# Mixture-of-experts stage of a two-layer model: two weight units split ahead of each border between experts, token products before the lists, one branch fewer

## The chip, the cores and the metric

The kernel runs on one core of one Trainium2 chip. The metric is the device time of one execution in microseconds (us). Five engines work side by side, each through its own list of instructions in order: PE multiplies matrices, DVE and ACT work on vectors and on activations, POOL does the slower elementwise work and issues gathers and scatters, SP issues loads. They wait for one another through semaphores.

## The reference, cut to what matters

Two layers on 512 tokens of width 1024. The stage that is changed is the expert layer of the first layer's second half: every token goes to the two best of eight experts, and an expert is a gated product of inner width 1408.

```python
D_MODEL = 1024
SEQ = 512
D_FF = 11 * D_MODEL // 4
N_EXPERTS = 8
TOP_K = 2
D_FF_EXPERT = D_FF // 2

def swiglu(x, w1, w3, w2):
    return (jax.nn.silu(x @ w1) * (x @ w3)) @ w2
```

The result of a token is the sum over its two experts of gate times `swiglu` with that expert's weights. All of it is float32.

## The kernel before, in words

**Products.** A float32 operand is split into a high part (`hi`, L76, on ACT) and a low part (`lo`, L79, on DVE, which subtracts the high part from the value); a product is three matmuls, low by high, high by low and high by high (L121 to L123). So every weight passes ACT and then DVE before PE can use it.

**Order and queues.** The code is written in one order; a scheduler then sets each engine's list, and `pin` keeps an instruction at its place. At run time each engine goes through its list in order.

**Weights.** An expert has 18 units of weights, 12 of them for the first two products (`w13`) and 6 for the last (`w2`); a unit is 1 MB at most. SP loads them through a ring of six places (`Stream.load`, L1216). `Stream.take` splits the next unit into tiles `wh` and `wl`, each half a unit, out of a pool of four pairs, and then lets SP load the unit six further on. One unit is outside this: the first unit of the next expert is split ahead into the tile `pre`, by `then()`, near the end of the expert before. With one block of tokens, a 1 MB unit is 12 matmuls of 512 columns on PE, two instructions on ACT and two on DVE.

**Experts and arms.** The experts are taken in order of their token counts. Each has three arms: one block of up to 128 tokens, a block and a half (the half block's products are folded, L1522, L1523), or two blocks. Two branches (L1698, L1701) choose the arm from a number, `codei`, that DVE works out and every engine loads (`values_load`). A `hint` ahead of each branch tells the sequencer which arm will come. In the profiled execution the experts 0, 2, 3, 5 and 6 have one block, and 1, 4 and 7 a block and a half. I call the change from expert e-1 to expert e border e. At a border ACT and DVE each copy half of the expert's output `y` out of PE's accumulators (L1625, L1626), go through the jump at the end of the arm (L1701), and then split the second unit of the next expert, in pieces of 512 columns (`fine`).

**Ahead of expert 0.** The normalised tokens come from PE as `pxn`; ACT and DVE split them into `nh` and `nl` (L1407, L1408), in two halves of the width (`hf`). `lists()` sorts the experts by size on DVE, ends with `codei`, and scatters the token lists with eight DMAs from POOL (L1352). `sums` are POOL's eight additions `nh+nl` (L1409), whose results ACT writes to `xn_d` with four DMAs (L1429); the gathers for the later experts read them. Expert 0's own tokens are picked by matmuls with one-hot matrices: 64 products `pO` (L1414, L1415), split into `xg` by ACT and DVE. Before, `lists()`, the split of `pre` and POOL's first four sums stand between the two halves.

**Behind expert 7.** A last branch (label `spill`, L1708) leads to code for more tokens than two blocks hold; all engines pass it before PE's `pyo` (L1733), which puts expert 7's rows back in place, and DVE's `y2` stage (L1735).

Of the kernel before, what the change touches and what calls it, by code (L numbers as in the profile page):

```python
# [48 lines left out]
class Core:  # L49
# [34 lines left out]
        self.nc.sync.dma_start(r, src)  # L84
        return self.split(r, k, n, dst, pin, eng, alone)

    def split(self, r, k, n, dst=None, pin=False, eng=None, alone=False, fine=False):

        kp = -(-k // 2)
        hs, ls = [], []  # L90
        for k0 in range(0, k, kp):
            s, m = k0 * n, (min(k0 + kp, k) - k0) * n
            if dst:
                h, l = (d[:, s:s + m] for d in dst)
            else:
                h = self.wpool.tile([128, 1024], FR, tag="wh", name="wh")[:, :m]
                l = self.wpool.tile([128, 1024], FR, tag="wl", name="wl")[:, :m]
            step = n if fine else m
            for c in (slice(o, o + step) for o in range(0, m, step)):
                q = r[:, s + c.start:s + c.stop]  # L100
                a = eng.tensor_copy(h[:, c], q) if alone else self.hi(h[:, c], q)
                b = self.lo(l[:, c], q, h[:, c], eng)
                self.last_split = a, b
                if pin:
                    self.tc.keep_in_program_order(a)
                    self.tc.keep_in_program_order(b)
            hs.append(h.rearrange("p (k n) -> p k n", n=n))
            ls.append(l.rearrange("p (k n) -> p k n", n=n))
        return Parts(hs, kp), Parts(ls, kp)
# [1066 lines left out]
    def _moe(self, m1, m2):  # L1176
# [33 lines left out]
        class Stream:  # L1210
# [7 lines left out]
            def take(st, late=False, **kw):  # L1218
                i = st.taken
                st.taken += 1  # L1220
                _, k, w = unit(*st.units[i])
                got = self.split(ring[(st.place + i) % 6][:, :k * w], k, w, **kw)
                if i + 6 < len(st.units) and not late:
                    st.load(i + 6)
                return got

        main = Stream([(e, n) for e in range(NE) for n in range(18)], 0)
        for i in range(3):
# [99 lines left out]
                pin(v.tensor_scalar(key[:, 1:], rank[:, 1:], float(r), -7 * 256.0, op0=OP.is_ge, op1=OP.mult))  # L1328
                pin(v.tensor_tensor(lam[:, 1:], lam[:, 1:], key[:, 1:], op=OP.add))

        def lists():
            sort()
            pin(v.tensor_scalar(t1, pos, 256.0, 2048.0 - 256.0, op0=OP.is_ge, op1=OP.mult))
            pin(v.tensor_tensor(t1, t1, lam[:, None, :].to_broadcast([128, 4, 8]), op=OP.add))
# [15 lines left out]
            for j in range(2):  # L1350
                for i in range(4):
                    st = g.indirect_dma_start(out=self.list_d[:, :],  # L1352
                                              out_offset=bass.IndirectOffsetOnAxis(ap=lii[:, j, i:i + 1], axis=0),
                                              in_=self.tid[:, i:i + 1], in_offset=None)
                    for o in scat:
                        tc.declare_no_dep(st.ins, o.ins, reason="every slot is written once")
                    scat.append(st)
            g.dma_start(lst, self.list_d.rearrange("(p c) o -> p (c o)", p=128))
            by = lambda t: t[:, None, :].to_broadcast([128, 8, 8])
            for src, dst in ((rc[:, 1], order), (cnt, None)):  # L1360
# [26 lines left out]
        def hint(e, after={}):  # L1387

            for t in mybir.ALL_ENGINES:
                with tc.issue_after(after[t].ins) if t in after else nullcontext():  # L1390
                    tc.mark_branch_hint_location(f"expert{e}" if e < NE else "spill", (code >> 3 * e + 2) & 1 if e < NE else 0,
                                                 engines=(t,))

        O = [self.bank("pp", "pO") for _ in range(3)] + [self.bank("pt", "pO")]
        for o in O:
            mm(o, self.z1[0:1].to_broadcast([1, 128]), self.z1[0:1].to_broadcast([1, 512]), start=True, stop=False)
        for hf in range(2):
            c = slice(512 * hf, 512 * hf + 512)
            ps, sums = [], []
            for i in range(4):  # L1400
                p = self.bank("pc", "pxn")
                mm(p, ident, rn[:, i, 4 * hf:4 * hf + 4, 0:128], start=True, stop=False)
                mm(p, rows[:, i * 128:(i + 1) * 128], self.gb[:, c], start=False, stop=True)
                ps.append(p)
            for i in range(4):
                col = rs[:, i:i + 1]
                nc.scalar.activation(nh[i][:, c], ps[i], AF.Copy, scale=col)  # L1407
                pin(v.scalar_tensor_tensor(nl[i][:, c], ps[i], col, nh[i][:, c].bitcast(FT), op0=OP.mult, op1=OP.subtract))  # L1408
                sums.append(lambda i=i, c=c: g.tensor_tensor(xn[:, i, c], nh[i][:, c].bitcast(FT), nl[i][:, c].bitcast(FT), op=OP.add))  # L1409
                for k in range(4):  # L1410
                    kk = 4 * hf + k
                    o = O[kk // 2][:, kk % 2 * 256:kk % 2 * 256 + 256]
                    ks = slice(kk * 128, kk * 128 + 128)
                    mm(o, nh[i][:, ks], hot[:, i], start=False, stop=False)  # L1414
                    mm(o, nl[i][:, ks], hot[:, i], start=False, stop=(i == 3 and k % 2 == 1))  # L1415
                if hf and i == 1:
                    code = nc.values_load(codei[0:1, 0:1], min_val=0, max_val=8 ** NE - 1)
                    hint(0)
            if not hf:
                lists()  # L1420
                main.take(dst=pre, pin=True, late=True)
            for add in sums:
                add()
            for j in range(2 * hf, 2 * hf + 2):
                th, tl = (XG[0][:, a, 2 * j:2 * j + 2].rearrange("p k b n -> p (k b n)") for a in range(2))
                self.hi(th, O[j])
                pin(self.lo(tl, O[j], th))
# [70 lines left out]
        def expert(e, blocks, xt, weights, start=None, nxt=None, first=(), then=None, extra=None, half=None):  # L1498
# [46 lines left out]
            for cc in range(6):  # L1545
# [16 lines left out]

                for u in range(2):
                    ahead = first and cc == u == 0
                    w = first if ahead else weights.take(pin=bool(mine) and cc == 1, fine=bool(first) and cc == 0)
                    for b in blocks:
                        if ahead and b and mine:
                            turn(mine, xt, 1, rows[1])
                        product(w, u, b)
# [15 lines left out]
            for u in range(6):  # L1585
# [12 lines left out]
                                      start=(kk == 0), stop=(kk == 10))  # L1598
                if u == 0:
                    flush(5, "pc")  # L1600
                if u == 3 and not over:
                    hint(e + 1, {mybir.EngineType.PE: last, mybir.EngineType.Activation: self.last_split[0],
                                 mybir.EngineType.DVE: self.last_split[1], mybir.EngineType.SP: weights.loaded})
                if nxt and u == (4 if e == 0 else 2):
# [51 lines left out]
                                         in_offset=bass.IndirectOffsetOnAxis(ap=ri[:, j, i:i + 1], axis=0))  # L1656
                    v.scalar_tensor_tensor(xn[:, i], d, wt[:, j, i:i + 1], xn[:, i], op0=OP.mult, op1=OP.add)

        first = [Parts([p.rearrange("p (k n) -> p k n", n=512)], 4) for p in pre]
        for e in range(NE):  # L1660
            if e == NE - 1:

                lo = m1.tile([128, 4, D], FT, tag="xg0", name="ylo")
                hi = [m2.tile([128, D], FT, tag=t, name="yhi") for t in ("y", "y", "xg", "xg")]
                for i in range(4):
                    for j, d in ((1, lo[:, i]), (0, hi[i])):
                        g.indirect_dma_start(out=d, out_offset=None, in_=self.y_d[0:1792, :],
                                             in_offset=bass.IndirectOffsetOnAxis(ap=rwi[:, j, i:i + 1], axis=0))
                start = None

                def nxt(_):
# [3 lines left out]
            else:  # L1675
                start = lambda e=e: fetch((0, 1) if e == NE - 2 else (0,), e + 1)
                nxt = lambda xs, e=e: turn(xs, XG[(e + 1) % 2])

            def then(e=e):
                if e + 1 < NE:  # L1680
                    main.take(dst=pre)
                    main.load(main.taken + 4)

            if e:
                for k in (e, min(e + 1, NE - 1)):
                    which(k)
            at, known = main.taken, dict(regs)
            extra = {1: gates, 3: rows_of_last}.get(e)
            arm_e = (code >> 3 * e) & 3

            def arm(a):
                main.taken = at
                regs.clear()
                regs.update(known)
                expert(e, (0, 1) if a else (0,), XG[e % 2], main, start, nxt, first, then, extra, 1 if a == 1 else None)


            with tc.If(arm_e == 1 - likely[e], preferred_fallthrough_block=False) as other:  # L1698
# [1 line left out]
            with other.Else():  # L1700
                with tc.If(arm_e > 1, label=f"expert{e}", preferred_fallthrough_block=True) as full:  # L1701
                    arm(2)
                with full.Else():
                    arm(likely[e])
            regs.clear()
            regs.update(known)

        with tc.If((code >> 3 * (NE - 1)) & 3 == 3, label="spill"):  # L1708
            others = Stream([(e, n) for e in range(NE) for n in range(18)], main.taken)
            for i in range(6):  # L1710
                others.load(i)
            xt = m1.tile([128, 2, 8, 2, 128], FR, tag="xg0", name="xg")
            for e in range(NE):
                spill(e, others, xt)


        y2 = m1.tile([128, 4, D], FT, tag="xg0", name="y2")
# [662 lines left out]
```

## Time and profile before

| | |
|---|---|
| time, median of 3 executions | 2525.89 us (2522.98 to 2527.27) |
| profiled execution: its own time / its span | 2531.56 us / 2529.7 us |
| mean granted TensorE clock | 0.955 |
| busy share of the span: PE, DVE, ACT, POOL | 93%, 67%, 47%, 19% |
| expert stage in the span | 1107.60 to 1670.00 us |

The span goes from the first to the last instruction of the profiled execution. PE is busy nearly all the time over the whole span; the expert stage takes 562 us of it. The shares are means over stages of different kinds, so the expert stage is read by itself, and there border by border.

### The profile page before, as it was taken

The page shows a single profiled execution, that of the slowest core. Times are in us where ns is not written, and L with a number is a line of the kernel's source. Part 1 is how long each engine was busy: PE and PEld are TensorE (multiplying, and loading weights), DVE is VectorE, ACT ScalarE, POOL GpSimd, SP SyncE. Part 2 cuts the span into 40 slices and gives each one's busy share as a digit, 9 for nine tenths or more (in the row PEclk, how much of TensorE's full clock was granted, in tenths as well). Part 3 has the DMA queues.
Part 4 walks back from the last instruction along what each step waited for, and adds up shares of the span by engine and source line. Part 5 has one row for each costly group of instructions (what it writes and reads, how often), then busy time and mean ns, then how long its engine had stood idle before and what let it go on. Part 6 is the DMA issues. An engine that isn't in the chain of part 4 may idle for free. (4 is left out here: it accounts for less than half of the span.)

```text
span 2529.7 us, 34883 instructions
## 1 busy us (share of the span) xinstructions
PE 2347.8 (93%) x12559; PEld 1901.6 (75%) x12559; DVE 1703.1 (67%) x3585; ACT 1193.1 (47%) x2155; POOL 473.5 (19%) x599
## 2 busy tenths in 40 slices
PE   8999998978999889988989998969999998999997
PEld 7899988866788867756767776758776778787776
DVE  5877668768854774366677677685786557578465
ACT  5544434322333423245565666545555445546453
POOL 1010123665676201030000000110001022001103
PEclk9999999989999899979999999989999998999998
DMA  4323222556645662256678588714131222223111
GB/s 162 112 79 96 62 84 101 202 176 217 236 167 196 183 176 82 102 183 260 230 292 317 175 307 326 280 60 147 55 104 61 95 84 90 79 75 104 59 51 67
DMA packets 107629, 375.34 MB, mean 148 GB/s; under 512 B 23202, under 2 KB 49218, under 8 KB 77448
## 3 DMA queue, kind: packets, MB, share of 16 engines
q1 hardware_dynamic: 73440, 285.86, 32.9%
q0 software_dynamic: 13552, 61.18, 7.0%
q10 hardware_dynamic: 20408, 25.48, 3.0%
q8 instruction: 115, 1.88, 0.3%
q14 instruction: 114, 0.93, 0.1%
HBM read 335.76 MB, written 36.72 MB: 147 GB/s over the span
## 5 line engine op out<-in xcount | busy, mean ns | idle before, releaser
L79 DVE TENSOR_TENSOR wl<-raw,wh 128x1024 fp32r<-128x1024 f32 (+4 forms) x248 | 295.3, 1194 | 202.5 <-ACT wh L76 198.4
L76 ACT ACTIVATE wh<-raw 128x1024 fp32r<-128x1024 f32 (+5 forms) x262 | 245.9, 947 | 285.0 <-PE pp L115 86.4
L79 DVE TENSOR_TENSOR wl<-ring,wh 128x1024 fp32r<-128x1024 f32 (+1 forms) x280 | 297.2, 1099 | 104.9 <-ACT wh L76 102.4
L115 PE MATMUL pp<-xl,wh 128*128 128x512 f32 (+1 forms) x944 | 350.1, 372 | 4.3 <-DVE xl L79 4.3
L114 PE MATMUL pp<-xh,wh 128*128 128x512 f32 (+1 forms) x944 | 349.7, 377 | 4.2 <-ACT wh L76 1.5
L116 PE MATMUL pp<-xh,wl 128*128 128x512 f32 (+1 forms) x944 | 347.8, 370 | 0.0
L76 ACT ACTIVATE wh<-ring 128x1024 fp32r<-128x1024 f32 (+1 forms) x280 | 256.3, 955 | 114.2 <-issue 45.9
L114 PEld LDWEIGHTS pp<-xh,wh 128*128 128x128 f32 x944 | 180.8, 194 | 38.2 <-issue 3.1
L115 PEld LDWEIGHTS pp<-xl,wh 128*128 128x128 f32 x944 | 182.6, 194 | 33.1 <-DVE xl L79 5.1
L116 PEld LDWEIGHTS pp<-xh,wl 128*128 128x128 f32 x944 | 182.4, 193 | 28.4 <-issue 1.8
L121 PE MATMUL ph<-wh,xg 128*128 128x512 f32 (+1 forms) x352 | 139.2, 407 | 30.1 <-ACT wh L76 30.0
L116 PE MATMUL pf<-xh,wl 128*128 128x512 f32 (+1 forms) x384 | 145.6, 380 | 4.4 <-DVE wl L79 4.4
L115 PE MATMUL pf<-xl,wh 128*128 128x512 f32 (+1 forms) x384 | 146.0, 381 | 1.5 <-DVE xl L79 1.5
L114 PE MATMUL pf<-xh,wh 128*128 128x512 f32 (+1 forms) x384 | 145.7, 381 | 1.1 <-ACT wh L76 0.6
L122 PE MATMUL ph<-wl,xg 128*128 128x512 f32 (+1 forms) x352 | 139.2, 395 | 1.8 <-DVE wl L79 1.8
L123 PE MATMUL ph<-wh,xg 128*128 128x512 f32 (+1 forms) x352 | 136.7, 389 | 0.0
L121 PEld LDWEIGHTS ph<-wh,xg 128*128 128x128 f32 x352 | 69.4, 201 | 46.4 <-ACT wh L76 34.1
L1832 DVE SCALAR_TENSOR_TENSOR adaacc<-adaraw,sc,adaacc 128x512 f32<-128x512 f32 x84 | 90.0, 1072 | 18.9 <-DMA adaraw<-w_ada 17.8
L1894 ACT ACTIVATE s<-s,sst 128x128 f32<-128x128 f32 (+3 forms) x128 | 71.0, 557 | 35.8 <-DVE sst L1892 34.0
L116 PEld LDWEIGHTS pf<-xh,wl 128*128 128x128 f32 x384 | 74.3, 194 | 17.7 <-DVE wl L79 4.8
L1479 POOL DMA_INDIRECT xgn<-xn_d,lst x10 | 11.1, 1109 | 402.5 <-PE pxg L1491 392.4
L1902 ACT ACTIVATE PT<-ptp 128x128 f32<-128x128 f32 (+3 forms) x128 | 51.8, 434 | 73.3 <-PE ptp L1899 58.4
(743 smaller groups left out, 5687.4 us busy)
## 6 DMA issues: line engine op xcount, KB each, us to landing
ring<-moe SPq DMA_DIRECT2D x120, 1024.0 KB, 6.1
raw<-w_in SPq DMA_DIRECT2D x30, 1024.0 KB, 4.8
adaraw<-w_ada POOLq DMA_DIRECT2D x24, 1024.0 KB
raw<-w SPq DMA_DIRECT2D x22, 1024.0 KB, 4.8
ring<-moe SPq DMA_DIRECT2D x24, 512.0 KB, 5.4
raw<-w SPq DMA_DIRECT2D x16, 704.0 KB, 3.9
raw<-w_glu SPq DMA_DIRECT2D x8, 1024.0 KB, 4.9
raw<-w_out SPq DMA_DIRECT2D x8, 1024.0 KB, 5.0
```

Source lines behind the costliest of these rows:

```text
L76: return self.nc.scalar.activation(dst, src, AF.Copy, **kw)
L79: return (eng or self.nc.vector).tensor_tensor(dst, src, hi.bitcast(FT), op=OP.subtract)
L114: mm(ps, wh, xh, start=start, stop=False)
L115: mm(ps, wh, xl, start=False, stop=False)
L116: return mm(ps, wl, xh, start=False, stop=stop)
L121: mm(ps, ah, wh, start=start, stop=False)
L122: mm(ps, ah, wl, start=False, stop=False)
L123: return mm(ps, al, wh, start=False, stop=stop)
L1479: g.indirect_dma_start(out=x, out_offset=None, in_=self.xn_d[:, :], in_offset=bass.IndirectOffsetOnAxis(ap=lst[:, q:q + 1], axis=0))
L1832: v.scalar_tensor_tensor(acc, r[:, k], s, acc, op0=OP.mult, op1=OP.add)
L1894: nc.scalar.activation(s, s, AF.Exp, scale=-1.0, bias=st[:, 0:1], accum_out=st[:, 1:2])
L1902: nc.scalar.activation(dst, src, AF.Copy)
```

## The change

1. **Two units ahead.** `then()` also takes the second unit of the next expert. It goes into one of four fixed pairs of tiles (`halves`), used in turn (`turned`) and kept over the arms. For expert 0 the second unit is taken before the token products. The pieces of 512 columns move from the second unit to the third.
2. **Token products whole.** All eight `nh` and `nl` come first, then `lists(sums)` and `pre`, then all 64 products. POOL does the eight scatters before the eight sums.
3. **No last branch.** The spill code moves into the full arm of expert 7, and so do the gathers and additions of the earlier rows into its arms.

```diff
-    def split(self, r, k, n, dst=None, pin=False, eng=None, alone=False, fine=False):
+    def split(self, r, k, n, dst=None, pin=False, eng=None, alone=False, fine=False, into=()):
...
+            elif into:
+                h, l = (d[:, :m] for d in into[len(hs)])
...
+                if "dst" not in kw:
+                    n = min(k, 2)
+                    kw["into"] = [halves[(turned[0] + j) % 4] for j in range(n)]
+                    turned[0] += n
...
+        halves = [[self.wpool.tile([128, 1024], FR, tag=t, name=t) for t in ("wh", "wl")] for _ in range(4)]
+        turned = [0]
...
-        def lists():
+        def lists(sums):
...
+            for dst, a, b in sums:
+                pin(g.tensor_tensor(dst, a, b, op=OP.add))
             g.dma_start(lst, self.list_d.rearrange("(p c) o -> p (c o)", p=128))
...
-                sums.append(lambda i=i, c=c: g.tensor_tensor(xn[:, i, c], nh[i][:, c].bitcast(FT), nl[i][:, c].bitcast(FT), op=OP.add))
+                sums.append((xn[:, i, c], nh[i][:, c].bitcast(FT), nl[i][:, c].bitcast(FT)))
+        lists(sums)
+        main.take(dst=pre, pin=True, late=True)
+        for hf in range(2):
+            for i in range(4):
...
-            if not hf:
-                lists()
-                main.take(dst=pre, pin=True, late=True)
-            for add in sums:
-                add()
...
-                    w = first if ahead else weights.take(pin=bool(mine) and cc == 1, fine=bool(first) and cc == 0)
+                    w = first[u] if first and cc == 0 else weights.take(pin=bool(mine) and cc == 1,
+                                                                        fine=bool(first) and cc == 1 and u == 0)
...
-                if u == 3 and not over:
+                if u == 3 and not over and e + 1 < NE:
...
-        first = [Parts([p.rearrange("p (k n) -> p k n", n=512)], 4) for p in pre]
+        begun = [Parts([p.rearrange("p (k n) -> p k n", n=512)], 4) for p in pre]
+        first = [begun, main.take()]
...
+            def then(e=e):
+                if e + 1 < NE:
+                    main.take(dst=pre)
+                    main.load(main.taken + 4)
+                    later.append(main.take())
...
+                    if e == NE - 1:
+                        with tc.If(arm_e == 3):
+                            others = Stream([(eo, n) for eo in range(NE) for n in range(18)], main.taken)
...
                 with full.Else():
                     arm(likely[e])
+            if later:
+                first = [begun, later[-1]]
...
-        with tc.If((code >> 3 * (NE - 1)) & 3 == 3, label="spill"):
```

The order of the instructions shows what that moves. First DVE, at the end of expert 2 and the start of expert 3's full arm as it stands in the program (border 3; the jump marks the border). The names: `wl` and `pre` are low parts of weights, `xg` of tokens, `hb` the gated products. Before:

```order
L79 TENSOR_TENSOR wl<-ring,wh 128x1024 x4
L1391 REGISTER_ALU x2
L2376 BRANCH_PREFETCH_HINT
L79 TENSOR_TENSOR wl<-ring,wh 128x1024 x2
L79 TENSOR_TENSOR xg<-pxg,xg 128x4x128 x2
L79 TENSOR_TENSOR wl<-ring,wh 128x1024
L1626 COPY y<-py 128x512 x2
L1701 UNCONDITIONAL_BRANCH
L79 TENSOR_TENSOR wl<-ring,wh 128x512 x4
```

Now:

```order
L79 TENSOR_TENSOR wl<-ring,wh 128x1024 x4
L1403 REGISTER_ALU x2
L2397 BRANCH_PREFETCH_HINT
L79 TENSOR_TENSOR wl<-ring,wh 128x1024 x2
L79 TENSOR_TENSOR xg<-pxg,xg 128x4x128 x2
L79 TENSOR_TENSOR wl<-ring,wh 128x1024 x3
L1638 COPY y<-py 128x512 x2
L1720 UNCONDITIONAL_BRANCH
```

Two low parts of 1024 columns, the next expert's second unit, now stand ahead of the copies of `y`; four pieces of 512 columns are gone from behind the jump. (The lists show the arm with two blocks; the copies are one for an engine in the arm that runs.) Next ACT, at a border into an arm with a block and a half (`sl` is the activation, `folds` the folded half block). Before:

```order
L1625 ACTIVATE y<-py 128x512 x2
L1631 DMA y_d<-y 128x1024 x2
L1701 UNCONDITIONAL_BRANCH
L76 ACTIVATE wh<-ring 128x512 x4
L1577 ACTIVATE sl<-ph 128x256
L76 ACTIVATE xg<-pxg 128x4x64 x2
L1522 ACTIVATE folds<-ph 64x512
L1577 ACTIVATE sl<-folds 64x256
L76 ACTIVATE wh<-ring 128x1024 x4
```

Now:

```order
L1637 ACTIVATE y<-py 128x512 x2
L1643 DMA y_d<-y 128x1024 x2
L1720 UNCONDITIONAL_BRANCH
L1589 ACTIVATE sl<-ph 128x256
L76 ACTIVATE xg<-pxg 128x4x64 x2
L1533 ACTIVATE folds<-ph 64x512
L1589 ACTIVATE sl<-folds 64x256
L76 ACTIVATE wh<-ring 128x512 x4
L76 ACTIVATE wh<-ring 128x1024 x2
```

The first weights that ACT splits behind the jump stand behind the fold now, and they are the third unit. Last POOL, between the token products and expert 0's branches. Before:

```order
L1409 TENSOR_TENSOR xn<-nh,nl 128x512 x4
L1352 DMA list_d<-tid,lii 4096x1 x8
L1417 TENSOR_LOAD codei
L1409 TENSOR_TENSOR xn<-nh,nl 128x512 x4
L1358 DMA lst<-list_d 128x32
```

Now:

```order
L1362 DMA list_d<-tid,lii 4096x1 x8
L1369 TENSOR_TENSOR xn<-nh,nl 128x512 x8
L1433 TENSOR_LOAD codei
L1370 DMA lst<-list_d 128x32
```

The first four sums have moved from ahead of the scatters to behind them; ACT's four DMAs to `xn_d` read the sums, and on ACT they now stand behind all four `xg` and ahead of expert 0's branches, as before.

## Rows read from the trace of the kernel before

**Rows 1.** Window of expert 3: length, busy PE PEld DVE ACT POOL, clock, DMA, GB/s.

```profile
1315.88:1374.40 58.52, 51.94 (x233) 40.72 (x230) 45.72 (x54) 38.12 (x52) 1.98 (x2) 0.94 0.85 314
```

**Rows 2.** Waits, 1164 to 1670 us: total, times, longest.

```profile
ACT wh L76 <- issue: 45.9, 12, 7.7
PE ph L121 <- ACT wh L76: 30.0, 9, 5.7
```

**Rows 3.** PE's timeline at borders 1 to 7: matmuls around the idle time.

```profile
1172.53 0.80 PE L121 MATMUL ph<-wh,xg 128*128 128x512 f32 x1 [5.74 <-ACT wh L76]
...
1266.29 0.80 PE L121 MATMUL ph<-wh,xg 128*128 128x512 f32 x1 [3.66 <-ACT wh L76]
...
1315.88 0.47 PE L121 MATMUL ph<-pre,xg 128*128 128x512 f32 x1
...
1324.11 0.79 PE L121 MATMUL ph<-wh,xg 128*128 128x512 f32 x1 [5.19 <-ACT wh L76]
...
1381.94 0.80 PE L121 MATMUL ph<-wh,xg 128*128 128x512 f32 x1 [4.61 <-ACT wh L76]
...
1474.59 0.50 PE L121 MATMUL ph<-wh,xg 128*128 128x512 f32 x1 [1.80 <-ACT wh L76]
...
1532.97 0.80 PE L121 MATMUL ph<-wh,xg 128*128 128x512 f32 x1 [5.26 <-ACT wh L76]
...
1591.36 0.49 PE L121 MATMUL ph<-wh,xg 128*128 128x512 f32 x1 [3.42 <-ACT wh L76]
```

**Rows 4.** Timeline of ACT and DVE at border 3 (1315.88 us).

```profile
1315.10 0.60 ACT L1625 ACTIVATE y<-py 128x512 f32<-128x512 f32 x1 [3.06 <-PE py L123]
1323.43 1.67 ACT L76 ACTIVATE wh<-ring 128x512 fp32r<-128x512 f32 x3 [7.73 <-issue]
...
1307.32 2.36 DVE L79 TENSOR_TENSOR pre<-ring,pre 128x1024 fp32r<-128x1024 f32 x2 [0.63 <-ACT pre L76]
...
1315.64 0.69 DVE L1626 COPY y<-py 128x512 f32<-128x512 f32 x1 [1.36 <-PE py L123]
1324.15 0.69 DVE L79 TENSOR_TENSOR wl<-ring,wh 128x512 fp32r<-128x512 f32 x1 [7.82 <-ACT wh L76]
```

**Rows 5.** Windows behind border 3's idle time, columns as in the first group.

```profile
1324.10:1330.00 5.90, 5.81 (x13) 3.86 (x14) 5.85 (x8) 4.48 (x6) 0.00 (x0) 0.53 0.19 33
1330.00:1345.00 15.00, 15.00 (x68) 12.15 (x67) 14.15 (x17) 12.09 (x16) 0.00 (x0) 1.00 0.88 334
```

**Rows 6.** The branch line L1701: ns min/median/max, first and last start.

```profile
L1701 PEldq COMPARE_BRANCH  x8: 367/443/4979, 1102.5 to 1582.5; - x8
```

**Rows 7.** Timeline ahead of expert 0 on PE, DVE, ACT and POOL.

```profile
1099.38 0.58 PE L1415 MATMUL pO<-hot,nl 128*128 128x256 f32 x1 [6.14 <-DVE nl L1408]
...
1107.63 0.65 PE L121 MATMUL ph<-pre,xg 128*128 128x512 f32 x1 [2.22 <-ACT wh L76]
...
1116.80 0.63 PE L121 MATMUL ph<-wh,xg 128*128 128x512 f32 x1
...
1081.38 0.20 DVE L1324 TENSOR_TENSOR pair<-key 128x49 f32<-128x49 f32 x1
...
1088.83 0.15 DVE L1377 CAST codei<-most 128x1 int32<-128x1 f32 x1
...
1087.68 0.69 ACT L1407 ACTIVATE nh<-pxn,rs 128x512 fp32r<-128x512 f32 x1 [2.47 <-PE pxn L1403]
...
1085.93 1.11 POOL L1352 DMA_INDIRECT list_d<-tid,lii  x1 [5.15 <-DVE pair L1361]
...
1095.08 0.97 POOL L1352 DMA_INDIRECT list_d<-tid,lii  x1 [0.30 <-issue]
1099.48 4.97 POOL L1409 TENSOR_TENSOR xn<-nh,nl 128x512 f32<-128x512 f32 x4 [3.43 <-DVE nl L1408]
```

**Rows 8.** Timeline behind expert 7 on PE and DVE.

```profile
1676.84 5.48 PE L1733 MATMUL pyo<-xg,hotT 128*128 128x512 f32 x14 [6.88 <-DVEq L1708]
...
1672.89 1.45 DVE L79 TENSOR_TENSOR xg<-folds,xg 64x512 fp32r<-64x512 f32 x2
```

More of the change, by code (lines that the diff above doesn't have):

```diff
@@ L1390, in hint @@
                 with tc.issue_after(after[t].ins) if t in after else nullcontext():
-                    tc.mark_branch_hint_location(f"expert{e}" if e < NE else "spill", (code >> 3 * e + 2) & 1 if e < NE else 0,
-                                                 engines=(t,))
+                    tc.mark_branch_hint_location(f"expert{e}", (code >> 3 * e + 2) & 1, engines=(t,))
         O = [self.bank("pp", "pO") for _ in range(3)] + [self.bank("pt", "pO")]
@@ L1396, in _moe @@
             mm(o, self.z1[0:1].to_broadcast([1, 128]), self.z1[0:1].to_broadcast([1, 512]), start=True, stop=False)
+        sums = []
         for hf in range(2):
             c = slice(512 * hf, 512 * hf + 512)
-            ps, sums = [], []
+            ps = []
             for i in range(4):
@@ L1657, in spill, with arm, earlier_rows @@
                     v.scalar_tensor_tensor(xn[:, i], d, wt[:, j, i:i + 1], xn[:, i], op0=OP.mult, op1=OP.add)
-        first = [Parts([p.rearrange("p (k n) -> p k n", n=512)], 4) for p in pre]
+        begun = [Parts([p.rearrange("p (k n) -> p k n", n=512)], 4) for p in pre]
+        first = [begun, main.take()]
         for e in range(NE):
-            if e == NE - 1:
+            if e < NE - 1:
+                start = lambda e=e: fetch((0, 1) if e == NE - 2 else (0,), e + 1)
+                nxt = lambda xs, e=e: turn(xs, XG[(e + 1) % 2])
+            else:
+                start = None
+            def then(e=e):
[3 more added lines that the diff above has]
+                    later.append(main.take())
+            if e:
+                for k in (e, min(e + 1, NE - 1)):
+                    which(k)
+            at, known = (main.taken, turned[0]), dict(regs)
+            extra = {1: gates, 3: rows_of_last}.get(e)
+            arm_e = (code >> 3 * e) & 3
+            later = []
+            def arm(a):
+                main.taken, turned[0] = at
+                regs.clear()
+                regs.update(known)
+                go_on = nxt if e < NE - 1 else earlier_rows()
+                expert(e, (0, 1) if a else (0,), XG[e % 2], main, start, go_on, first, then, extra, 1 if a == 1 else None)
+            def earlier_rows():
                 lo = m1.tile([128, 4, D], FT, tag="xg0", name="ylo")
@@ L1668, in _moe, with add @@
                                              in_offset=bass.IndirectOffsetOnAxis(ap=rwi[:, j, i:i + 1], axis=0))
-                start = None
-                def nxt(_):
+                def add(_):
                     for i in range(4):
@@ L1674, in nxt @@
                             pin(v.scalar_tensor_tensor(xn[:, i], d, rest[:, j, i:i + 1], xn[:, i], op0=OP.mult, op1=OP.add))
[L1675 to L1695, printed above, removed]
+                return add
             with tc.If(arm_e == 1 - likely[e], preferred_fallthrough_block=False) as other:
@@ L1702, in _moe @@
                     arm(2)
+                    if e == NE - 1:
+                        with tc.If(arm_e == 3):
+                            others = Stream([(eo, n) for eo in range(NE) for n in range(18)], main.taken)
+                            for i in range(6):
+                                others.load(i)
+                            xt = m1.tile([128, 2, 8, 2, 128], FR, tag="xg0", name="xg")
+                            for eo in range(NE):
+                                spill(eo, others, xt)
                 with full.Else():
                     arm(likely[e])
+            if later:
+                first = [begun, later[-1]]
             regs.clear()
             regs.update(known)
-        with tc.If((code >> 3 * (NE - 1)) & 3 == 3, label="spill"):
[L1709 to L1714, printed above, removed]
         y2 = m1.tile([128, 4, D], FT, tag="xg0", name="y2")
```

## The prediction

> **What bounds the kernel now.** I read the shares of busy time first: PE is busy 93% of the span, so the time can fall only where PE idles or runs slowly. Then I took a window of one expert. Expert 3 lasts 58.52 us; PE is busy 51.94 us of it, DVE 45.72, ACT 38.12 [rows 1]. PE leads, but DVE has only 12.8 us of slack, and 7.82 us of that is one wait at the border [rows 4]; some 5.0 us are left to speed DVE up. Next came the list of waits in the expert stage: the largest that PE has is `ph` waiting for ACT's `wh`, 30.0 us in nine waits; beside it ACT idles 45.9 us "by issue", with nothing that the profile shows to wait for [rows 2].
>
> The timeline says where those are. At each border PE does the unit split ahead, then stands: 5.74, 3.66, 5.19, 4.61, 1.80, 5.26 and 3.42 us at borders 1 to 7, 29.7 in all [rows 3]. At border 3 PE begins expert 3 at 1315.88 and idles from 1324.11 - 5.19 = 1318.92, so one unit covers 3.04 us. ACT meanwhile copied `y` at 1315.10 and has its next instruction, the second unit's split, at 1323.43, after 7.73 us of idle time; DVE waits 7.82 us for ACT [rows 4]. ACT lacks no data there: what comes between is the jump at the end of the arm. I read it as time to get the next code. [...]
>
> **Two units ahead.** The number of splits, loads and matmuls stays; their place changes. ACT's two instructions (2.0 us, by DVE's rows for `pre` at most 2.36) stand ahead of its copy of `y`, where it idles 3.06 us: free. On DVE two low parts of `pre`'s size take 2.36 us, and DVE idles 1.36 us ahead of its copy [rows 4]. So its copy, and the jump queued behind, come 1.0 us later at the five borders behind one-block experts (1, 3, 4, 6, 7). ACT's jump does not wait for that copy, and DVE idles until ACT has split something, so a late DVE costs between 0 and 1.0 us a border; I take 0.5 at border 4 and leave it inside border 1's figure.
>
> PE now has two units, 6.1 us, before it needs anything from behind the jump. A wait of s becomes s - 3.04. That saves 3.0 at each of borders 2, 3 and 6, all of border 5's 1.8, and 3.0 - 0.5 = 2.5 at border 4. At border 7 the arm has a block and a half, with both units used for both, so all 3.42 can go. Border 4 has such an arm too, but ACT must first split the half block's `xg` there, behind the jump. At border 1 ACT has the gates' small work as well ahead of that; PE would reach the half block about as early as ACT has it, and I take 1.0 of the 3.0. Sum: 1.0 + 3.0 + 3.0 + 2.5 + 1.8 + 3.0 + 3.4 = 17.7 us; bounds 0 (the wait only moves) and 29.7 (all of it goes).
>
> The clock: 13 matmuls at the rate of the full level (15.00/68 = 0.22 us) take 2.9 us instead of 5.90, so a border costs 3.0 us through it. It can stay up only where no idle time is left, borders 5 and 7 and perhaps 2: between 0 and 9. But in these 5.90 us DVE is busy 5.85 us [rows 5], so a faster PE would soon wait for DVE. I take 2.0.
>
> What the row shows of ACT's idle time at the jump differs by border; border 5's was short, as PE's 1.80 us there says [rows 3]. [...]
>
> **Token products whole.** PE's 6.14 us wait for `nl` goes, since `nl` no longer stands behind the lists [rows 7]. In exchange the lists start when the last `nh` (1087.68 + 0.69) and `nl` (as long) are there, about 1089.1, not 1081.38; they take 7.6 us (to 1088.98), so `codei` is there at 1096.7. PE's first 32 products ended at 1099.38 - 6.14 = 1093.24, so the rest end well before 1102; then PE's branch, which is the one that lasts 4.98 us in the branch rows [rows 6], starts behind `codei` and ends about 1102, where before the first `ph` was at 1107.63 [rows 7]. PE has two units then; the first took 1116.80 - 1107.63 = 9.2 us, with a wait in it, and 12 more matmuls at the lower level take 12 x 5.90/13 = 5.4: the third is needed about 1117, where before the second began at 1116.80. Is it there? POOL's first scatter came 4.55 us behind the lists' start, now at 1093.7; the eight last 1096.05 - 1085.93 = 10.1 us, to 1103.8, and the eight sums, now behind them, 2 x 4.97, to 1113.7 [rows 7]. ACT's DMAs to `xn_d` wait for them, and behind those in ACT's queue stands its branch and the split of the third unit. So it is there at about 1116 with a quick branch, or 1121 if ACT waits some 5 us for code as at a border. One unit more done by 1117 is worth between 3.04 and 5.4; late by 5, it is -2. I take +2.5, bounds -2.5 and +5.4.
>
> **No last branch.** PE idles 6.88 us ahead of `pyo`, until every engine is through the branch; DVE's last low part that it needs ends at 1672.89 + 1.45 = 1674.34, PE starts at 1676.84 [rows 8]. If all of `pyo` waits for that part, 2.5 us are saved; if the full block's rows can go first, up to 6.9. I take 3.5. The additions of earlier rows are the same work on the same engine. The loads keep their number, one more of them ahead of each border; DMA's share in expert 3 is 0.85 [rows 1], so they cost nothing as long as the ring stays ahead.
>
> **Sum.** 17.7 + 2.0 + 2.5 + 3.5 = 25.7 us. From the profiled execution's own 2531.56 us that gives 2505.9; it stands 5.7 us above the median of the runs, and from the median, 2525.89, it gives **2500 us**.
>
> **Rivals.** A measurement here can tell about 0.2%, 5 us, from no change.
> - *The wait moves.* PE reaches the same wait one unit later, and what it gained is given back, since DVE has those 5 us of slack an expert and no more. For: DVE is busy all through the time behind a border [rows 5]. Against: DVE needs 2.36 us a unit, PE 3.04, so DVE gains on PE unit by unit. Left: borders 5 and 7 (5.2), start 2.5, tail 3.5, together 11.2: 2515 us.
> - *It hardly pays.* That, with the start at -2.5, the tail at 2.5 and border 5 as long as the others: 3.4 - 2.5 + 2.5 = 3.4 us, 2522 us. ACT queued behind POOL's sums speaks for it.
> - *PE waits for code itself* (slower). PE's own jump took 4.98 us at its longest of eight and 0.44 at the median [rows 6]. The change moves PE's code, and puts the spill block ahead of expert 7's short arm. If the hint comes too late at all borders, each costs 4.5 us that nothing covers: 31.8 us, against 25.7 saved: 2532 us. It decides from six borders on. Against: the hint keeps its place ahead of the jump, and seven of eight were short. [...]
> - *The clock stays up.* If what is left of the waits no longer drops the clock, 7 x 3.0 us come back instead of 2.0: 44.7 saved, 2481 us. Against: four borders keep 2 us or more of idle time, and DVE's load.
>
> **Chances and range.** Forecast 0.60, the moved wait 0.13, hardly any gain 0.09, PE's code 0.09, the clock 0.09. Faster: 0.60 + 0.13 + 0.09 = 0.82; same 0.09; slower 0.09. The forecast's own range is 2490 to 2510; the range that leaves out the clock and PE's code, 0.18, is 2486 to 2524.
>
> **What would show it.** Right: PE's waits for `wh` near 1 to 3 us at borders 1, 3, 4 and 6, none at 5 and 7, and now on the third unit, with ACT still idle some 7 us at the jump; DVE's copy of `y` about 1 us late; expert 3 near 55 us; PE's first `ph` about 5 us sooner against the last `pxn`; no join ahead of `pyo`. Wrong: waits of the old length on the third unit; PE idle at `codei` or the branch for over 5 us; ACT's first split of expert 0 far behind 1116; PE's branch rows at 5 us throughout.

## The result and the profile after

The changed kernel takes 2491.38 us (2490.89 to 2496.5, 4 runs) against 2525.45 us; the ratio is 0.987, 95% interval 0.9853 to 0.9887, so 28 to 37 us are saved. The forecast was 2500 us, in a range from 2486 to 2524.

The profiled execution has a span of 2494.6 us, 35.1 us less than that of before. First the page's line of busy time, then three experts as windows (length, then busy PE, PEld, DVE, ACT, POOL, granted clock, DMA share, GB/s): experts 3, 4 and 6.

```profile
PE 2334.6 (94%) x12559; PEld 1893.1 (76%) x12559; DVE 1700.2 (68%) x3585; ACT 1194.8 (48%) x2155; POOL 485.0 (19%) x599
...
1302.81:1359.63 56.82, 52.44 (x233) 41.20 (x231) 45.38 (x55) 38.29 (x52) 1.93 (x2) 0.94 0.90 333
1359.63:1449.56 89.93, 84.13 (x389) 63.67 (x389) 54.80 (x74) 47.31 (x74) 0.94 (x1) 0.98 0.64 234
1500.43:1556.10 55.67, 51.20 (x238) 41.20 (x238) 44.91 (x54) 39.33 (x55) 1.88 (x1) 0.97 0.92 348
```

Expert 3 is 1.7 us shorter than in [rows 1], with nearly the same busy time on every engine. The waits of the expert stage (total, times, longest) answer to [rows 2]:

```profile
ACT wh L76 <- issue: 44.9, 15, 8.0
...
PE ph L123 <- ACT wh L76: 8.3, 4, 3.2
```

PE's wait for `wh` went from 30.0 to 8.3 us, while ACT idles as long at its jumps as before, 44.9 us: ACT's waits are covered, not removed. Waits that PE has in their place, for the half blocks, do not show in this line. PE's timeline at borders 1 to 7, as in [rows 3]:

```profile
1166.80 0.48 PE L1543 MATMUL phT<-cst,hb 128*128 128x128 f32 x1 [5.93 <-DVE hb L1591]
...
1256.38 0.50 PE L123 MATMUL ph<-wh,xg 128*128 128x512 f32 x1 [1.46 <-ACT wh L76]
...
1311.22 0.50 PE L123 MATMUL ph<-wh,xg 128*128 128x512 f32 x1 [2.59 <-ACT wh L76]
...
1365.11 0.50 PE L125 MATMUL ph<-wh,xg 128*128 128x512 f32 x1 [1.35 <-issue]
1369.39 0.44 PE L1543 MATMUL phT<-cst,hb 128*128 128x128 f32 x2 [1.77 <-DVE hb L1591]
...
1456.39 0.50 PE L123 MATMUL ph<-wh,xg 128*128 128x512 f32 x1 [1.08 <-ACT wh L76]
...
1509.32 0.50 PE L123 MATMUL ph<-wh,xg 128*128 128x512 f32 x1 [3.17 <-ACT wh L76]
...
1563.05 0.47 PE L1527 MATMUL ph<-pre,xg 128*128 128x512 f32 x1 [2.28 <-DVE xg L1519]
```

The waits at borders 2, 3, 5 and 6 are on the third unit now, each shorter than before. At borders 1 and 4 PE waits for the half block's gated products (`hb`), and at border 1 it stands as long for them, 5.93 us, as it stood for the second unit before, 5.74. At border 7 it waits for DVE's copy of the half block's tokens, and DVE's timeline there shows why that copy is late:

```profile
1557.69 0.68 DVE L1638 COPY y<-py 128x512 f32<-128x512 f32 x1
1562.48 0.43 DVE L1519 CAST xg<-xg 128x512 fp32r<-128x512 f32 x1 [4.11 <-issue]
```

Between the two stands DVE's own jump, with nothing that the profile shows to wait for.

The places that do not belong to a border are expert 0's start and the end of expert 7 (timelines of PE, POOL, ACT and DVE, as in [rows 7] and [rows 8]):

```profile
1094.93 0.77 PE L123 MATMUL ph<-pre,xg 128*128 128x512 f32 x1 [3.75 <-issue]
...
1108.71 0.50 PE L123 MATMUL ph<-wh,xg 128*128 128x512 f32 x1 [2.82 <-ACT wh L76]
...
1097.00 9.89 POOL L1369 TENSOR_TENSOR xn<-nh,nl 128x512 f32<-128x512 f32 x8
...
1103.20 4.04 ACTq L1440 DMA_DIRECT2D xn_d<-xn  x4
1108.03 3.15 ACT L76 ACTIVATE wh<-ring 128x512 fp32r<-128x512 f32 x5 [16.20 <-issue]
...
1643.28 0.50 PE L1754 MATMUL pyo<-xg,hotT 128*128 128x512 f32 x1 [1.91 <-ACT xg L76]
...
1644.29 1.45 DVE L79 TENSOR_TENSOR xg<-folds,xg 64x512 fp32r<-64x512 f32 x2
```

ACT computes nothing for 16.20 us ahead of its first split behind expert 0's branch, the third unit: it has the DMAs to `xn_d` to issue, and POOL's eight sums end only at 1106.9. Behind expert 7, PE begins `pyo` 1.91 us after its last product, and 2.5 us before DVE's last low part ends at 1645.74.

One gain stands where I expected none. The stage ahead of the experts, from the first product of the S5 mixer (`pu`) to the last `prn`, took 236.47 us in the profile of before and 229.90 us in that of after. The windows, before, before a second time (the experiment below), after:

```profile
829.50:1065.97 236.47, 217.96 (x1573) 178.43 (x1574) 124.38 (x212) 75.03 (x125) 20.77 (x29) 0.94 0.46 132
```

```profile
830.10:1062.70 232.60, 214.08 (x1572) 175.81 (x1573) 124.48 (x212) 75.08 (x125) 20.53 (x29) 0.96 0.47 134
```

```profile
828.90:1058.80 229.90, 213.87 (x1573) 176.16 (x1574) 126.65 (x214) 77.03 (x127) 21.40 (x29) 0.96 0.49 140
```

The kernel before itself varies by 3.9 us here from one execution to the next, and the kernels below that have only part two or only part three of the change took 230.7 and 230.3 us in this stage. So the short stage is not the work of the second unit ahead. I compare the profiles from the last `prn` on, where the change is.

### The profile page after: what moved, and what is told of

Same layout as the page of the kernel before. It is cut to its first block, busy times and chain, and to the rows that moved or that the text cites. A ratio compares the mean times of both kernels' runs of the same rounds, so it can differ in the third digit from the quotient of the medians.

```text
span 2494.6 us, 34874 instructions
## 1 busy us (share of the span) xinstructions
PE 2334.6 (94%) x12559; PEld 1893.1 (76%) x12559; DVE 1700.2 (68%) x3585; ACT 1194.8 (48%) x2155; POOL 485.0 (19%) x599
## 4 chain that ended last, share of the span: by engine, by line
PE 59%; DVE 11%; DMA 4%; issue 4%; ACT 2%; POOL 2%; ACTq 0%; DVEq 0%; POOLq 0%; SPq 0%
PE pp L116 6%; PE pp L117 6%; PE pp L118 6%; PE ph L124 3%; PE ph L123 3%; PE ph L125 3%; DVE wl L79 3%; PE pf L116 2%; PE pf L117 2%; PE pf L118 2%; PE pv L1932 2%; DVE adaacc L1853 2%; PE ph L1528 1%; PE ptp L1920 1%; PE pglu L116 1%
## 5 line engine op out<-in xcount | busy, mean ns | idle before, releaser
L118 PEld LDWEIGHTS pp<-xh,wl 128*128 128x128 f32 x944 | 182.0, 193 | 28.3 <-issue 1.8
L1490 POOL DMA_INDIRECT xgn<-xn_d,lst x10 | 19.1, 1906 | 375.8 <-PE pxg L1502 367.3
```

The costliest lines, as they stand in the source:

```text
L118: return mm(ps, wl, xh, start=False, stop=stop)
```

## The experiments

**The kernel before and the changed kernel again.** No edit.

> The kernel before once more, for the stage ahead of the experts, where the changed kernel's profile is 6.5 us shorter (PE's waits at 919, 935 and 942 us of the profile before) though the diff touches nothing there but one split and one load. Theory: those waits hang on when small loads land and vary from one execution to the next, so this profile's stretch from 895 to 985 us may come out several us shorter or longer than the one shown, and the ratio is 1 within 0.2%. Rival: they belong to the program; then this profile repeats them within 1 us.

> The changed kernel once more, beside the three that follow. Both theories: ratio 0.985 to 0.989, and a profile that repeats the first one from expert 0 on within some 3 us.

Measured: 2523.83 us, ratio 0.9995 (0.9979 to 1.001); and 2493.39 us, ratio 0.9898 (0.9874 to 0.9922), in a later comparison. The S5 stage of before was 3.9 us shorter the second time (rows above): the theory of small loads landing early or late is borne out as far as variation goes; that the loads are its cause was only argued. The changed kernel's second ratio lies just above the 0.985 to 0.989 that was expected, within its interval, and its profile repeats the first within 2.5 us. With this, the profiles compare as follows (from the last `prn` to the first product behind the experts `pp`; from the last `prn` to expert 0's first `ph`; then the length of each expert, the last one up to `pyo`; worked out from PE's rows, us):

```
                  prn-pp  prn-e0     e0     e1     e2     e3     e4     e5     e6     e7
before             635.4    41.7   56.2   95.9   56.1   58.5   95.5   54.9   58.3   93.8
before, again      634.7    41.0   56.7   95.6   57.0   57.7   95.6   54.1   57.3   94.8
two ahead alone    604.9    41.7   55.7   92.7   51.7   55.4   87.1   53.5   54.7   88.0
whole alone        636.9    36.5   62.4   95.9   57.5   57.9   95.8   54.0   57.6   94.9
no branch alone    631.0    42.1   56.1   97.4   57.3   58.2   95.4   54.2   57.5   89.3
changed kernel     608.0    36.1   59.5   94.9   53.5   56.8   89.9   50.9   55.7   87.2
changed, again     605.5    36.1   60.4   93.0   54.4   56.3   87.4   53.9   54.4   85.9
```

**The three parts, each alone on the kernel before.** Their edits are the three parts of the diff above: `halves`, `first[u]` and the second `main.take()`; `lists(sums)` behind both halves; the moved spill code. (What the second part puts ahead of the lists are the splits `nh` and `nl`; in the code the products stand behind the lists, other than the title has it.)

> The kernel before with the first part alone: two units ahead of each border and of expert 0, lists and last branch as before. Theory (the sum of the prediction as the trace after bears it out): the borders give 19 us and expert 0's second unit some 2 to 3, so about 2504 us, ratio 0.991. Rival 1: the stage ahead of the experts became shorter because of this part (the added split and load stand there): 6.5 us more, about 2498. Rival 2: the borders' gain needs the other parts: over 2512.

> The kernel before with the second part alone: products whole, lists behind, scatters ahead of the sums. Theory: PE starts expert 0 some 5 us sooner, but with one unit ahead it needs the second at once, and ACT reaches it only behind POOL's eight sums, so PE idles there and the part alone gives between 2 us faster and 4 us slower, ratio 0.999 to 1.002. Rival: the removed wait for the low parts is worth its 6 us: about 2519.5.

> The kernel before with the third part alone: no last branch. Theory: 6 us as in the trace after, since the full block's rows go first: about 2519.5 us, ratio 0.9976. Rival 1: 2.5 us, as if all products behind expert 7 waited for the last low part. Rival 2: nothing, or a loss at border 7, since the spill code now lies ahead of expert 7's short arm.

Measured: 2500.12 us, ratio 0.9906 (0.9882 to 0.9931); 2525.52 us, 1.0012 (0.9994 to 1.0029); 2517.32 us, 0.9972 (0.9958 to 0.9987). By 2523 us these are 23.7 us saved, 3.0 lost or nothing, and 7.1 saved. Two units ahead are most of the gain (its interval is 17 to 30 us, and the profile, taken of the fastest of its four runs, shows the upper end). The rival that it shortens the stage ahead of the experts falls: 232.9 us there in its profile, against 230.3 and 230.7 without it. The products whole pay nothing alone: PE starts expert 0 some 5 us sooner, and expert 0 lasts 6 us longer. Without the last branch expert 7 is 4.5 to 5.5 us shorter in the profile, and the rival of 2.5 us is the less likely one. The rival of a loss at border 7 is borne out inside that gain. PE and DVE there, with part three alone:

```profile
1585.53 0.77 PE L1515 MATMUL ph<-pre,xg 128*128 128x512 f32 x1 [4.52 <-DVE xg L1507]
...
1584.96 0.43 DVE L1507 CAST xg<-xg 128x512 fp32r<-128x512 f32 x1 [6.20 <-issue]
```

With the last branch, DVE's next instruction stands 0.48 us behind its jump at border 7 (0.51 with two units ahead alone); without it, 5.3 to 6.3 us in every profile. PE's wait there is 3.42 us before, 4.52 with part three alone, none with part one alone and 2.28 in the changed kernel.

**Parts one and three without the second.**

> Parts one and three without the second (half of the products, the lists and four of POOL's sums in their old order). Theory: by the traces the second part costs about as much behind the branch as it gains ahead of it (PE starts expert 0 some 5 us sooner, expert 0 lasts 3 us longer in the changed kernel, and 6 us longer with the second part alone), so leaving it out changes the time by less than 3 us either way, ratio 0.985 to 0.989. Rival 1: the parts only sum up to their gain together, the second being worth 5 us where two units are ahead: ratio 0.989 or 0.990. Rival 2: the second part is a loss here too: 0.984 or less.

Measured: 2489.42 us, ratio 0.9872 (0.9849 to 0.9894), beside 0.9898 of the changed kernel, measured with it. The intervals overlap: the second part is worth nothing that these runs can tell.

**ACT freed of the DMAs at expert 0.**

```diff
-            nc.scalar.dma_start(self.xn_d[i * 128:(i + 1) * 128, :], xn[:, i])
+            g.dma_start(self.xn_d[i * 128:(i + 1) * 128, :], xn[:, i])
```

> The changed kernel with the four DMAs to xn_d issued by POOL, behind its sums, and no more by ACT ahead of expert 0's branch. Theory: PE's wait for the third unit of expert 0 (2.82 us at 1105.89 us of the profile after) is ACT standing behind POOL's sums; ACT then takes its branch some 10 us sooner, the wait is gone, and PE gains 2.8 us and up to 1.5 us of clock, ratio 0.001 to 0.002 below the changed kernel's. Rival: ACT waits for the code behind the branch all the same, or DVE's low parts are late as well: no change within 1 us in that stretch.

Measured: 2489.65 us, ratio 0.9879 (0.9858 to 0.99). ACT and the weights (waits from 1095 to 1165 us of its profile):

```profile
ACT pre L76 <- DMA ring<-moe: 4.4, 1, 4.4
...
PE py L123 <- ACT wh L76: 3.1, 1, 3.1
```

The ratio is 0.0019 below the changed kernel's, as the theory said, but the intervals overlap, and the profile shows no gain. ACT split the third unit 15 us sooner, and the wait of 2.82 us is gone, as the theory said. But expert 0 lasts 60.61 us as before (59.46 and 60.42), about what the rival expected, for another reason than the rival's: PE waits 3.1 us at 1147.09, 38 us further on, where ACT waits for a load. The ring's sixth place is memory that `nl` uses until POOL's sums have read it, so SP can issue that load only at 1104.44 in the changed kernel, at 1106.12 here, and at 1097.62 with parts one and three alone. The later loads stand behind it in SP's list, and from 1110 to 1145 us the DMA share is 1.01. So once ACT is free, the loads that began late bound expert 0. With parts one and three, where they began sooner, expert 0 lasts 56.5 us; no run moved that load alone.

**The output copied by DVE, so that ACT jumps early.**

```diff
-                    nc.scalar.activation(y[:, :512], py[b][0], AF.Copy)
+                    v.tensor_copy(y[:, :512], py[b][0])
                     v.tensor_copy(y[:, 512:], py[b][1])
...
-                    nc.scalar.dma_start(self.y_d[o:o + r, :], y[:r])
+                    g.dma_start(self.y_d[o:o + r, :], y[:r])
```

> The changed kernel with both halves of an expert's output copied by DVE and stored by a DMA of POOL's, so that ACT goes through the jump right behind its last split and does not wait for PE's last product. Theory: what is left of PE's waits for the third unit at borders 3 and 6 (2.6 and 3.2 us in the profile after) is ACT's time behind the jump, 5.5 us counted from the jump; the jump comes about 2 us sooner, so these waits shrink by 2 us or go, and borders 1 and 4 gain 1 to 2 us: 5 to 8 us in all with some clock, about 2485 us, ratio 0.983 or 0.984. Rival 1: DVE, with 0.7 us more to do at its busiest place, becomes the one that PE waits for: no gain, or 2 us lost. Rival 2: loading sets the pace in experts 3 and 6 (DMA share 0.90 and 0.93 in the profile after): the waits at the border shrink, but those two experts last as long as before.

Measured: 2491.54 us, ratio 0.9886 (0.9866 to 0.9905): no gain in the time, though the waits at borders 2, 3, 5 and 6 are gone and experts 2, 3, 5, 6 last 49.3, 51.7, 50.0 and 51.7 us, 203 together against 217 and 219. The second rival falls with that; expert 3's window in this profile:

```profile
1299.27:1350.94 51.67, 49.48 (x232) 39.15 (x231) 45.45 (x56) 38.15 (x51) 1.58 (x2) 1.00 0.95 354
```

The same loads come in 51.67 us at a DMA share of 0.95, where the changed kernel took 56.82 at 0.90, so the loads were not the pace there. The first rival gave the right time for a wrong reason: PE's waits for DVE's low parts are 0.5 to 1.0 us at borders 3 and 6. The gain was lost again in expert 4, 95.57 us. PE's and POOL's timelines at its start, then POOL's in the changed kernel:

```profile
1364.01 1.11 PE L1502 MATMUL pxg<-cst,xgn 64*128 64x64 f32 x8 [5.49 <-DMA xgn<-xn_d,lst]
...
1353.49 0.56 POOL L1643 DMA_DIRECT2D y_d<-y  x1 [47.83 <-DVE y L1638]
1356.73 0.98 POOL L1490 DMA_INDIRECT xgn<-xn_d,lst  x1 [2.67 <-issue]
```

```profile
1351.26 0.94 POOL L1490 DMA_INDIRECT xgn<-xn_d,lst  x1 [56.10 <-PE pxg L1502]
```

POOL waits for DVE's copy to store it, then jumps, and only then gathers the half block's tokens, 6 us behind the border (1350.94). In the changed kernel POOL has no store to wait for and takes that jump long before the others; the gather was issued at 1351.26, behind PE's `pxg`, 8 us ahead of the border. The same edit with the store on SP:

```diff
-                    nc.scalar.dma_start(self.y_d[o:o + r, :], y[:r])
+                    nc.sync.dma_start(self.y_d[o:o + r, :], y[:r])
```

> The changed kernel with the output copied by DVE, as before, and stored by a DMA of SP's, so that POOL can issue the gather for the half block of expert 4 ahead of the border, as in the changed kernel. Theory: the waits for the third unit stay gone at borders 2, 3, 5 and 6 (experts 2, 3, 5, 6 together 203 us as with the store on POOL, against 217 and 219 in the changed kernel's two profiles), and expert 4 is back from 95.6 to 88 or 90 us: from the normalised tokens to the projection behind the experts about 600 us, ratio 0.983 or 0.984. Rival: the loads behind SP's store start later at each border, and experts 3 and 6 wait for them: 205 us become 212 or more.

> The same copies and store on the kernel with parts one and three alone. Theory: the gains add up, since the token products and the borders do not touch: that stretch about 594 us (605.7 without the edit, less the 12 us of the four experts), ratio 0.980 to 0.982, the fastest of all. Rival: what the second part costs is luck of one profile; then it is as fast as the kernel beside it, within 2 us.

Measured: **2478.62 us, ratio 0.9803 (0.9779 to 0.9827)**, and 2481.54 us, 0.982 (0.9797 to 0.9843): both faster than the changed kernel's 0.9898 and 0.987, the first somewhat more so than the 0.983 expected, and one as fast as the other within their intervals, so that the second part makes no difference here either; the rival of the second expectation holds, and not its theory that this kernel is the fastest of all. In the profiles, as in the table above (the 605.7 us that the expectation gives for parts one and three are 599.2 up to the first `pp`):

```
                  prn-pp  prn-e0     e0     e1     e2     e3     e4     e5     e6     e7
one and three      599.2    35.3   56.5   95.3   54.0   55.7   87.8   51.0   54.0   85.8
copy DVE, POOL     599.0    35.5   60.6   94.2   49.3   51.7   95.6   50.0   51.7   86.8
copy DVE, SP       592.1    35.7   60.5   90.7   53.5   53.4   86.6   51.1   49.9   86.8
one, three, SP     592.3    41.0   58.0   91.0   50.3   54.0   86.8   51.6   48.9   87.0
```

Expert 4 is back at 86.6 us. Experts 2, 3, 5 and 6 take 208 and 205 us together, between the theory's 203 and the rival's 212: at border 2 a wait of 1.46 us for ACT's third unit is left in the first of the two. Border 3 in the same profile, ACT, then DVE and PE:

```profile
1303.95 2.19 ACT L76 ACTIVATE wh<-ring 128x512 fp32r<-128x512 f32 x4 [4.04 <-PE ph L124]
...
1302.43 0.68 DVE L1637 COPY y<-py 128x512 f32<-128x512 f32 x1
1303.03 0.68 DVE L1638 COPY y<-py 128x512 f32<-128x512 f32 x1
1307.96 0.69 DVE L79 TENSOR_TENSOR wl<-ring,wh 128x512 fp32r<-128x512 f32 x1 [4.25 <-ACT wh L76]
...
1308.71 0.50 PE L124 MATMUL ph<-wl,xg 128*128 128x512 f32 x1 [0.81 <-DVE wl L79]
```

ACT's first split comes 2.1 us after the border at 1301.84; in the changed kernel it came 7.7 us after it (1310.54 against 1302.81). The profile puts the 4.04 us ahead of it down to PE, but ACT's own records read otherwise. Its branch ends at 1298.49, 3.4 us ahead of the border, and the next instruction of its sequencer, a test of a semaphore that lasts 0.04 us, stands at 1303.79, 5.3 us later. In the changed kernel the branch ends at 1304.99, behind the copy of `y` and behind the store's DMA, which waits for DVE's half, and 5.5 us go by as well. So the jump takes as long as before; it begins 5.5 us sooner against the border, and PE's two units cover it. What is left of PE's waits at this border, 0.81 us and once 0.96, is DVE's, whose own jump takes from 1302.06 to 1307.87.

**No hints.** The call of `hint(e + 1, ...)` is left out.

> The changed kernel without the hints ahead of borders 1 to 7. The prediction's slower rival needs PE to wait some 5 us at each jump, as at expert 0. Theory: the hints are what keeps PE's jumps at 0.4 us; without them PE idles 3 to 5 us at most of the seven borders, with nothing to cover it, and the kernel is 15 to 35 us slower than with them, 2505 to 2525 us. Rival: the hints do nothing for PE; its branch rows stay at 0.4 us and the time at 2491.

Measured: 2511.97 us in one run, 18 to 21 us more than the changed kernel's medians, as the theory said. The edit takes the hints from all engines, so the time is not PE's alone. The branch rows (ns min/median/max) and PE's waits in the expert stage:

```profile
L1719 PEldq COMPARE_BRANCH  x8: 3282/6087/6686, 1089.5 to 1567.8; - x8
```

```profile
PE ph L123 <- issue: 34.5, 7, 12.7
...
PE pq L148 <- issue: 5.7, 1, 5.7
```

With the hints the same row reads as follows (the changed kernel):

```profile
L1720 PEldq COMPARE_BRANCH  x8: 352/445/3717, 1091.0 to 1555.5; - x8
```

The shortest of the eight, 3282 ns, is expert 0's, whose hint stays; the seven without a hint take 5.8 to 6.7 us. With the hints two of the eight are long, expert 0's (3717) and border 2's (3115), and the other six take 0.35 to 0.47 us.

So PE's jumps took 5.8 to 6.7 us each where no hint was given, and six of the seven took 0.35 to 0.47 us where one was; what the long ones wait for, no run shows. The price that the slower rival put on a late hint, 4.5 us a border that nothing covers, is half borne out: PE idles 2.3 to 12.7 us at the seven borders, 5.6 on average, but the time grew by some 2.8 a border, since behind such a jump PE no longer waits for ACT's third unit (8.3 us in the changed kernel, none here). The rival's condition, a hint that comes too late everywhere, did not come about.

## Why the prediction came out right

From the last `prn` to the products behind the experts, the two profiles of before and the two of after differ by 28.3 us on average, 27.2 of them up to `pyo`; 25.7 were forecast. By its terms, as means of the two profiles each:

- **Borders**: 17.7 + 2.0 forecast. Experts 1 to 6 give 1.8, 2.6, 1.5, 6.9, 2.1 and 2.8 us, and expert 7, whose 7.8 us hold some 5.0 of the last branch, 2.8: together 20.5. The mechanism was right: ACT's wait at the jump stays as long in total (45.9 us before, 44.9 after), two units cover more of it. The sizes were off one by one, and that the sum came so near is in part luck.
- **Border by border**: at border 1 the wait went over to the half block, 5.93 us for 5.74, where the prediction had PE reach it about as early as ACT has it. Border 3 gave half of its 3.0, and expert 3 took 56.8 and 56.3 us, not some 55: PE's idle time in it fell by 2.2 us (6.58 to 4.38 by the windows), and its busy time grew by 0.5. Border 4 gave 6.9 for 2.5: the granted clock in the first 25 us of expert 4 was 0.93 in one profile and 1.00 in the other, where it had been 0.83 in both profiles of before. The prediction had put the clock's gain at borders 5 and 7, and only where no idle time is left; here it stood at 1.00 with waits of 1.62, 0.55 and 2.30 us left. Border 7 still has 2.28 us of idle time. All 3.42 go there with part one alone, as forecast; what is left comes from part three, which put DVE's jump (4.11 us idle) ahead of its copy of the half block's tokens. The prediction took no such cost into its term for the last branch.
- **Border 5**: all of its 1.80 us were forecast to go; the profiles show waits of 1.08 and 2.77 us, and ACT's idle time at that jump, 2.72 us before, is 5.12 and 6.81 now. The short jump of before did not stay short.
- **Start**: +2.5 forecast; from the last `prn` to the end of expert 0 it was 1.8 us. PE's first `ph` came 5.3 us sooner and ACT's split at 1108.03, ahead of which it stood behind POOL's sums, as worked out. What was missed is the ring's sixth load. Part two is worth nothing measurable, by itself or on top of the others, so a part of the change that I put at a gain was none.
- **Last branch**: 3.5 forecast; 5.0 in the profiles (PE's wait ahead of `pyo` went from 6.88 to 1.91 us; with that part alone expert 7 is 5.0 shorter than the mean of before), 7.1 (3.3 to 10.6) in the runs of that part alone. The share of expert 7's gain that belongs to this part is an estimate, since the parts do not add up there: part one alone makes expert 7 shorter by 6.3 us, part three alone by 5.0, and the changed kernel by 7.8. Of the two bounds, 2.5 and 6.9, the upper was nearer, since the full block's rows go first.

Of the rivals, the moved wait falls: the one-block experts 2, 3, 5 and 6 each became shorter, and DVE did keep up; it came true at border 1 alone. The rival that has PE wait for code falls, as six of PE's seven jumps took 0.35 to 0.47 us. (The prediction read seven of eight of PE's branches as short. Two were long: border 2's took 1.95 us before and 3.1 now, though PE did not idle for it.) No run shows the 2.0 us of the clock by itself (its full and its lower level are the clocks 1.00 and 0.53 of [rows 5]); what the windows show in its place is that the clock did come back in part: in experts 4 (0.95 to 0.98), 2 and 6 (0.94 to 0.97) and 5 (0.97 to 1.00), and not in 1, 3 and 7. The timed runs saved 33 us (28 to 37) and 26 us (20 to 32) by their ratios; the profiles' 28.3 lie between the two.

What stays open: why expert 0's start took 35.3 us from the last `prn` in the kernel with parts one and three, and 41.0 to 42.1 us in the others that keep the old order there (to the end of expert 0 it is 91.8 us there and 97.4 to 99.0 in those others); and why expert 3's busy time grew.

## What to carry to other kernels

A wait at a jump can be covered by work made ready ahead of it (PE's waits for `wh` went from 30.0 to 8.3 us here), and further by letting the engine reach its jump early (ACT's began 5.5 us sooner at border 3). An engine that copies the last result has the jump behind that copy in its list, so give the copy to an engine that isn't waited for behind the jump, and the store to a queue in which nothing urgent stands behind it (expert 4 lasted 95.6 us with the store on POOL, 86.6 on SP). Before crediting a reordering, look for the memory that the moved work holds longer: here a ring's place, whose load was issued at 1104.44 us and at 1097.62 without the reordering. Where the profile names an engine that was done long before, look at the waiting engine's own branch. And take a second profile of the kernel before: a stage that nobody touched moved by 3.9 us.

## What the runs showed of the hardware

PE's jump took 0.35 to 0.47 us with a hint at six of the seven borders; at border 2, also with one, 1.95 us before and 3.12 in the changed kernel; ahead of expert 0, also with one, 4.98 and 3.72; and 5.8 to 6.7 at the seven borders of the kernel without hints. ACT's did not follow its hint in that way: from the end of its branch to its next instruction it took 0.4 to 5.6 us at the borders of the changed kernel and 0.4 to 6.5 in the kernel without hints (border 4 left out, where the next instruction waits for PE). Reached early or late, it took 5.3 and 5.5 us at border 3. That the time goes into getting code was argued and not shown. In the 3 us behind each of the seven waits of before, 1.80 to 5.74 us long, the granted clock was 0.50 to 0.80. In the changed kernel it was 0.66 behind a wait of 1.46 us (border 2) and 1.00 behind one of 1.08 us (border 5), and over the first 25 us of expert 4 it was 0.93 in one execution and 1.00 in the other.
